# Latent attention in a two-layer trunk: two heads taken together, exponentials and values in fp32, the two heads' value matmuls on the two halves of the array's columns

## The chip, the cores and the metric

The kernel runs on one core of a Trainium2 chip. The metric is the time of the device for one launch, in microseconds (us), as the median of several runs of the same program. Engines are named as the profile names them: PE is TensorE (PEld its weight loads), DVE is VectorE, ACT is ScalarE, POOL is GpSimd, SP is SyncE, which here only issues transfers.

## The reference, cut to what matters

Two layers run for 1024 latent tokens and 128 context tokens. The first layer (windowed attention beside a state-space scan) is not touched. The second is multi-head latent attention with 16 heads: queries and keys have 64 plain and 32 rotated elements per head, values have 64.

```python
def dense_attention(q, k, v, scale, sink=None):          # one block of 128 queries after the other
    s = jnp.einsum("bqhgd,bkhd->bhgqk", qblk, k).astype(jnp.float32) * scale
    p = jax.nn.softmax(s, axis=-1)
    return jnp.einsum("bhgqk,bkhd->bqhgd", p.astype(v.dtype), v)

def mla_attend(q, k, v, g, w_out):
    out = dense_attention(q[:, :, :, None, :], k, v, MLA_SCALE)
    return (out.reshape(b, L, MLA_WIDTH) * jax.nn.silu(g)) @ w_out
```

Latent queries see 1024 latent and 128 cached context keys (nine tiles of 128 keys); the 128 context queries see 128 context keys of their own. All inputs and outputs are float32.

## The kernel before, in words

TensorE takes two formats here. A *float32r* operand is rounded to the precision of one pass through the array. Where more is needed the kernel keeps a value as two such parts, hi and lo, with hi + lo equal to the value, and adds two or three products (`mm3`, L256 to L258, is hi·hi + hi·lo + lo·hi). A plain *fp32* operand is split by the machine itself: each fp32 matmul of the program stands in the trace as two MATMUL records with two weight loads.

Latent attention works head by head. Four operand sets (`AK`, `BK`, `AQ`, `BQ`: hi and lo of keys and queries, elements by tokens) hold two pairs of heads. For a head, `head_max` (L1428) first makes the scores' row maxima from a one-pass product `pp`, 24 products of 128 queries by 384 keys and one of 128, each reduced by a DVE TENSOR_REDUCE (shown as L209, the line of a helper) in the step after; the negated maximum goes by DMA into row 96 of `AQ`, so that the score product subtracts it.

`head_main` then walks the queries in chunks of 512, 512 and 128, and in a chunk the tiles of 128 keys. One *step* is one tile of keys of one head: three score matmuls (L1449 to L1451) into a PSUM bank `sc` of the ring `pre` (two banks); on ACT two exponentials of that bank, one rounded to float32r (`ph`, L1458) and one in fp32 (`pf`, L1459); on DVE `pl = pf - ph` (L1473); on POOL the running sum of `pf` for the denominator (L1477). One step later come two value matmuls (L1467, L1468), `V·ph` and `V·pl`, into one bank `acco`. `V` holds 64 hi and 64 lo columns, so that the bank's upper 64 rows are the part that belongs to the lo columns. At the end of a chunk `gather` adds the two halves of the bank (ACT copy L1489, DVE add L1490), sums the denominator over the partitions with a product by ones (`den`, L1496, fp32, one weight column), inverts it by way of DRAM, and multiplies by the gate.

Beside the steps run pieces of work for the next pair of heads: `operands` (projections by `mm3` into the other two operand sets, `place`), `quad_weights`, `quad_rope`, `quad_values` every fourth head, and `head_max`. `spread` deals them out over the steps, at most three or four PSUM banks (`mm`, `tr`) a step, and `Steps` puts off what follows. While one head of a pair is worked on, the maxima of the following head are made.

The code's order is not the final order. The tile framework orders the instructions of each engine by its own simulation of the program (`schedule_with_timeline_sim=True` at the end of the file) within the dependencies. Only what goes through `pinned` stays behind the instructions given to its engine before. Each engine then works strictly in the order so found.

SBUF is four large tiles, R, S, G, F (`Memory`), from which named rings of buffers are cut.

Of the kernel before, what the change touches and what calls it, by code (L numbers as in the profile page):

```python
# [20 lines left out]
D = 1024  # L21
# [59 lines left out]
class Segment:  # L81
    """columns of one SBUF tile, handed out and taken back while the kernel is traced"""
# [27 lines left out]
class Memory:  # L110
    """four tiles of SBUF: R holds operands of float32r products, F everything else, S and G either by turns"""
# [26 lines left out]
class Space:  # L138
    """named rings of buffers in the memory"""
# [53 lines left out]
class Steps:  # L193
    """pieces of work put off by a number of steps of the stream that they go along with"""
# [26 lines left out]
def hybrid_trunk(ctx: ExitStack, tc: tile.TileContext, I, O, dbg=None, stage=99):  # L221
# [23 lines left out]
    def split(hi, lo, src, scale=None, lo_eng=None):  # L245
        """hi + lo == src * scale exactly; scale is None, a power of two or a [P, 1] operand."""
        lo_eng = lo_eng or dve
        if scale is None:
            act.copy(hi, src)  # L249
            lo_eng.tensor_tensor(lo, src, hi.bitcast(F32), ALU.subtract)  # L250
# [92 lines left out]
    def modulation(sp, l, j, parts):  # L343
        """columns 256 j .. 256 j + 255 of the map of layer l; whole weights, or split ones where TensorE has no time to spare"""
# [43 lines left out]
    def rstd_of(p, ssq, n, width):  # L388
        """ssq [128, width] -> (ssq / n + eps) ** -0.5"""
# [11 lines left out]
    def weave(main, n_main, aux, n_aux):  # L401
        """n_aux steps of aux spread evenly over n_main steps of main"""
# [300 lines left out]
    def fm_proj(w, b, hT, c):  # L703
        """128 columns of a slab for a chunk of tokens, columns by tokens"""
# [66 lines left out]
    def chunk_states(p, fb, xt, Bt):  # L771
        """states of two heads before every chunk, forward ones at rows 0..63, backward ones, counted from the last chunk, below"""
# [271 lines left out]
    def norm_T(p, l, cond, xh, tok):  # L1044
        """modulated transpose of a normalised token tile"""
# [10 lines left out]
    def residual(p, half, acc, x, gate, adder=pool):  # L1056
        """x[:, half] += gate * acc"""
# [212 lines left out]
    def pinned(f, *a):  # L1270
        """an instruction that stays behind those that its engine was given before"""
# [4 lines left out]
    def spare(name):  # L1276
        """a bank, to be read in the next step"""
# [6 lines left out]
    def until(n):  # L1284
        """waits for the n-th step from now"""
# [49 lines left out]
    def quad_rope(Q):  # L1335
        """the rotated parts of four heads' queries"""
        qh, ql = quads[Q][0]
        rh = p7.tile([128, T], F32R, tag="qrh", name="qrh", at="G")
        rl = p7.tile([128, T], F32R, tag="qrl", name="qrl", at="G")
# [47 lines left out]
    def operands(pair):  # L1387
        """fills the operand sets of a pair of heads"""
# [11 lines left out]
    def head_max(h):  # L1400
        """row of -max of the scores, a group of query tiles at a time"""
# [35 lines left out]
    def head_main(h, op, chunks=CHUNKS):  # L1437
        """a step per tile of keys: its scores and exponentials; the values of the tile before"""
        s, a = h % NSET, h % 2
        for q0, n, kts in chunks:  # L1440
            qs = slice(q0, q0 + n)
            acc = []
            last = chunks is not CHUNKS
            total = p7.tile([128, n if last else 512], F32, tag=f"pt{n if last else 512}", name="pt1", bufs=2)[:, 0:n]
            first = None
            for i, kt in enumerate(kts):
                sc = psum("pre", "sc")
                ks = slice(kt * 128, (kt + 1) * 128)
                pe.matmul(sc[:, 0:n], AK[s][0:96, ks], BQ[s][:, qs], start=True, stop=False)  # L1449
                pe.matmul(sc[:, 0:n], BK[s][:, ks], AQ[s][0:96, qs], start=False, stop=False)  # L1450
                pe.matmul(sc[:, 0:n], AK[s][:, ks], AQ[s][:, qs], start=False, stop=True)  # L1451
                if behind:
                    behind[0]()
                steps.tick()
                pf = p7.tile([128, 512], F32, tag="pf", name="pf", bufs=3)[:, 0:n]
                ph = p7.tile([128, 512], F32R, tag="ph", name="ph", bufs=3)[:, 0:n]
                pl = p7.tile([128, 512], F32R, tag="pl", name="pl", bufs=2)[:, 0:n]
                act.activation(ph, sc[:, 0:n], AF.Exp, scale=SCALE_M)  # L1458
                act.activation(pf, sc[:, 0:n], AF.Exp, scale=SCALE_M)  # L1459
                yield  # L1460
# [3 lines left out]
                def values(V=quads[h // 4][2][h // 2 % 2][:, kt, a], ph=ph, pl=pl, acc=acc, total=total, i=i, last=i == len(kts) - 1, q0=q0, n=n):  # L1464
                    if i == 0:
                        acc.append(psum("o", "acco")[:, 0:n])
                    pe.matmul(acc[0], V, ph, start=(i == 0), stop=False)  # L1467
                    pe.matmul(acc[0], V, pl, start=False, stop=last)  # L1468
                    if last:
                        after(1, gather, h, op, q0, n, acc[0], total)  # L1470

                def rest(pf=pf, ph=ph, pl=pl, total=total, i=i, alone=len(kts) == 1, first=first, values=values):
                    dve.tensor_tensor(pl, pf, ph.bitcast(F32), ALU.subtract)  # L1473
                    if alone:
                        pool.tensor_copy(total, pf)
                    elif i > 0:
                        pool.tensor_tensor(total, first if i == 1 else total, pf, ALU.add)  # L1477
                    behind[0] = values
                behind.append(rest)
                first = pf  # L1480
# [3 lines left out]
    def gather(h, op, q0, n, acc, total):  # L1484
        """adds the two parts of a head's outputs; divides a pair of heads by the denominators, gates"""
        a, j = h % 2, h // 2
        qs = slice(q0, q0 + n)
        low = p7.tile([64, 512], F32, tag="ol1", name="ol1")[:, 0:n]
# [211 lines left out]
```

## Time and profile before

| what | before |
|---|---|
| median of 3 runs | 1939.34 us (1937.37 to 1945.99) |
| profiled execution: span from first to last instruction (the page has no other time of it) | 1936.3 us |
| what lies between that span and the median | 3.0 us |
| PE busy, share of the span | 1770.5 us, 91% |
| DVE busy | 1338.3 us, 69% |
| ACT busy | 972.3 us, 50% |
| POOL busy | 849.1 us, 44% |
| the latent attention's steps: first score to last denominator | about 1140 to 1838 us, 698 us |
| in that stretch: PE, DVE, ACT, POOL busy | 625.61, 647.57, 444.40, 451.75 us |
| granted TensorE clock in that stretch | 0.95 |

In views of instructions a row gives the line, engine and operation, `out<-in`, shapes and the count, then busy time and mean ns of one. A matmul's duration holds its way through the array as well, so neighbours overlap: what one costs PE is the distance from its start to the next one's start, which the view in order of time gives. That view merges neighbours of one kind into a row with a count.

### The profile page before, as it was taken

Reading aid. Unit: us, or ns where it says so; the run is one execution under the profiler, and the core shown is the slowest. Engines: PE = TensorE matmul, PEld = TensorE weight load, DVE = VectorE, ACT = ScalarE, POOL = GpSimd, SP = SyncE. Lnnn points to the kernel's source line nnn. Section 1 sums busy time; section 2 is a strip of 40 time slices with the busy share of each in tenths; the row PEclk is TensorE's granted clock in tenths of the full one; section 3 lists DMA queues with packets and bytes.
Section 4 is the critical chain, followed back from the end, with each engine's and each line's share of the span. In section 5 each row is a group of like instructions: output and inputs, shape, how many; then the busy total and the mean of one; then the engine's idle time right before and its main releaser. Section 6 shows DMA issues by size and latency. Waiting matters only on the chain. (4 is left out here: it accounts for less than half of the span.)

```text
span 1936.3 us, 28171 instructions
## 1 busy us (share of the span) xinstructions
PE 1770.5 (91%) x9031; PEld 1405.9 (73%) x9031; DVE 1338.3 (69%) x2421; ACT 972.3 (50%) x2201; POOL 849.1 (44%) x781
## 2 busy tenths in 40 slices
PE   7899999999987898989999999998989899988898
PEld 3899999868766866767788986666666566654586
DVE  5666455654544577676654359999999899999833
ACT  5533224655654454444344236666567566765521
POOL 3410000233443346566340105866775586765632
PEclk9999999999988888989999989999989899998999
DMA  7333333343436786554535320211120121112352
GB/s 256 111 91 111 93 105 104 118 121 98 127 110 186 232 262 212 167 185 157 170 89 177 107 64 12 60 27 38 33 60 19 40 63 30 33 40 89 91 168 87
DMA packets 210664, 210.33 MB, mean 109 GB/s; under 512 B 36162, under 2 KB 175504, under 8 KB 210516
## 3 DMA queue, kind: packets, MB, share of 16 engines
q1 hardware_dynamic: 210372, 208.40, 35.7%
q8 instruction: 72, 1.18, 0.3%
q14 instruction: 76, 0.62, 0.1%
q0 software_dynamic: 144, 0.13, 0.0%
HBM read 151.94 MB, written 51.72 MB: 105 GB/s over the span
## 5 line engine op out<-in xcount | busy, mean ns | idle before, releaser
L1477 POOL TENSOR_TENSOR arenaF<-arenaF 128x512 f32<-128x512 f32 x256 | 390.9, 1528 | 171.4 <-PE den L1496 96.0
L256 PE MATMUL acc<-arenaR 128*128 128x384 f32 (+4 forms) x1152 | 390.6, 340 | 14.4 <-ACT arenaR L252 4.7
L257 PE MATMUL acc<-arenaR 128*128 128x384 f32 (+3 forms) x1080 | 362.7, 336 | 0.1
L258 PE MATMUL acc<-arenaR 128*128 128x384 f32 (+4 forms) x1056 | 352.1, 335 | 0.8 <-DVE arenaR L250 0.6
L256 PEld LDWEIGHTS acc<-arenaR 128*128 128x128 f32 x1152 | 224.3, 195 | 41.2 <-issue 7.0
L209 DVE TENSOR_REDUCE arenaF<-pp 128x1 f32<-128x384 f32 (+1 forms) x400 | 204.0, 534 | 21.6 <-PE pp L1428 18.9
L257 PEld LDWEIGHTS acc<-arenaR 128*128 128x128 f32 x1080 | 210.0, 194 | 10.7 <-issue 1.8
L258 PEld LDWEIGHTS acc<-arenaR 128*128 128x128 f32 x1056 | 206.0, 195 | 13.2 <-issue 3.0
L1473 DVE TENSOR_TENSOR arenaG<-arenaF,arenaS 128x512 fp32r<-128x512 f32 (+1 forms) x202 | 200.0, 996 | 3.9 <-PE acco L1468 2.7
L1459 ACT ACTIVATE arenaF<-sc 128x512 f32<-128x512 f32 (+1 forms) x304 | 174.3, 576 | 7.3 <-POOL arenaF L1477 6.7
L1468 PE MATMUL acco<-arenaG 128*128 128x512 f32 (+1 forms) x304 | 134.1, 444 | 42.9 <-DVE arenaG L1473 38.5
L1458 ACT ACTIVATE arenaS<-sc 128x512 fp32r<-128x512 f32 (+1 forms) x202 | 117.3, 582 | 91.0 <-PE sc L1451 46.1
L1005 ACT ACTIVATE arenaG<-arenaG,arenaF 128x128 f32<-128x128 f32 x288 | 88.4, 389 | 115.9 <-POOL arenaG L1003 115.4
L250 DVE TENSOR_TENSOR arenaR<-arenaF,arenaR 128x512 fp32r<-128x512 f32 (+2 forms) x135 | 115.3, 869 | 41.9 <-ACT arenaR L249 35.5
L249 ACT CAST arenaR<-arenaF 128x512 fp32r<-128x512 f32 (+3 forms) x151 | 91.6, 625 | 81.2 <-DMA arenaF<-in_ab_w_in_dram 19.1
L1468 PEld LDWEIGHTS acco<-arenaG 128*128 128x128 f32 x304 | 59.5, 196 | 98.7 <-DVE arenaG L1473 88.1
L258 PE MATMUL acc<-arenaR,arenaS 128*128 128x512 f32 (+1 forms) x336 | 128.9, 387 | 0.0
L749 POOL TENSOR_TENSOR arenaG<-arenaF,arenaG 128x512 fp32r<-128x512 f32 x28 | 48.6, 1734 | 151.4 <-PE acco L753 83.4
L1428 PE MATMUL pp<-arenaR 96*128 96x384 f32 x300 | 104.3, 385 | 8.4 <-DVE arenaF L209 4.2
L256 PE MATMUL acc<-arenaR,arenaS 128*128 128x512 f32 (+1 forms) x264 | 106.3, 403 | 1.0 <-ACT arenaS L249 0.7
L257 PE MATMUL acc<-arenaR,arenaS 128*128 128x512 f32 (+1 forms) x264 | 105.4, 399 | 0.0
L1449 PE MATMUL sc<-arenaR 96*128 96x512 f32 (+1 forms) x228 | 96.5, 423 | 7.1 <-ACT arenaF L1459 6.9
(339 smaller groups left out, 4052.9 us busy)
## 6 DMA issues: line engine op xcount, KB each, us to landing
arenaF<-in_ada_w_dram SPq DMA_DIRECT2D x96, 256.0 KB
arenaG<-cum_d SPq DMA_DIRECT2D x36, 512.0 KB
arenaF<-in_ab_w_in_dram SPq DMA_DIRECT2D x51, 256.0 KB
z_d<-arenaF SPq DMA_DIRECT2D x36, 128.0 KB
xs_d<-arenaF SPq DMA_DIRECT2D x8, 576.0 KB
arenaF<-xs_d SPq DMA_DIRECT2D x9, 512.0 KB
arenaF<-z_d SPq DMA_DIRECT2D x9, 512.0 KB
x_d<-arenaG SPq DMA_DIRECT2D x9, 512.0 KB
```

What stands on the lines that cost most here:

```text
L209: f()
L250: lo_eng.tensor_tensor(lo, src, hi.bitcast(F32), ALU.subtract)
L256: pe.matmul(out, ah, bh, start=first, stop=False)
L257: pe.matmul(out, ah, bl, start=False, stop=False)
L258: pe.matmul(out, al, bh, start=False, stop=last)
L1428: pe.matmul(pp[:, 0:w], AQ[s][0:96, t * 128:(t + 1) * 128], AK[s][0:96, k0:k0 + w], start=True, stop=True)
L1449: pe.matmul(sc[:, 0:n], AK[s][0:96, ks], BQ[s][:, qs], start=True, stop=False)
L1458: act.activation(ph, sc[:, 0:n], AF.Exp, scale=SCALE_M)
L1459: act.activation(pf, sc[:, 0:n], AF.Exp, scale=SCALE_M)
L1468: pe.matmul(acc[0], V, pl, start=False, stop=last)
L1473: dve.tensor_tensor(pl, pf, ph.bitcast(F32), ALU.subtract)
L1477: pool.tensor_tensor(total, first if i == 1 else total, pf, ALU.add)
```

## The change

- `head_main` becomes `pair_main`: a step is still one tile of keys of one head, but the two heads of a pair alternate, tile by tile.
- One exponential a step is left, in fp32 (L1455 of the changed file). The rounded one and the DVE subtraction are gone.
- `V` is kept in fp32: 64 columns a head. `quad_values` copies it out of PSUM with one ACT copy where it made a hi and a lo part.
- The value product is one fp32 matmul a step (L1465) in place of two float32r ones. The first head's goes to rows 0 to 63 of the bank `acco`, the second head's to rows 64 to 127: 64 columns of the array each. The code writes the two one behind the other, once per tile of keys of the pair.
- `gather` works once per pair and chunk: one ACT copy of the whole bank, no DVE add; the denominators of both heads go to rows 0 and 64 of one bank. The product of gate and reciprocal moves from POOL to DVE. For the short chunk POOL's copy is gone.
- The maxima of the next pair's two heads both come from the 12th step of a pair's 36 on, and those of the first pair's two heads both ahead of the first step (before: 19 of 50 products ahead).
- Buffers: `pf` six deep in G, which is set to fp32; `vv` half as wide, the rotated queries in F, and the residual stage's input ring in G.

The core of the diff:

```diff
         for pr in range(2):
-            tiles.append(p7.tile([128, NKT, 2, 128], F32R, tag="vv", name="vv", bufs=3, at="G"))
+            tiles.append(p7.tile([128, NKT, 2, 64], F32, tag="vv", name="vv", bufs=3, at="G"))
...
             for pr in range(2):
-                v = tiles[pr][:, kt]
-                after(1, split, v[:, :, 0:64], v[:, :, 64:128], acc[:, pr * 128:(pr + 1) * 128].rearrange("p (a d) -> p a d", a=2))
+                after(1, act.copy, tiles[pr][:, kt], acc[:, pr * 128:(pr + 1) * 128].rearrange("p (a d) -> p a d", a=2))
...
-                act.activation(ph, sc[:, 0:n], AF.Exp, scale=SCALE_M)
-                act.activation(pf, sc[:, 0:n], AF.Exp, scale=SCALE_M)
-                yield
+                for a in range(2):
+                    s = (2 * j + a) % NSET
+                    sc = psum("pre", "sc")
+                    pe.matmul(sc[:, 0:n], AK[s][0:96, ks], BQ[s][:, qs], start=True, stop=False)
+                    pe.matmul(sc[:, 0:n], BK[s][:, ks], AQ[s][0:96, qs], start=False, stop=False)
+                    pe.matmul(sc[:, 0:n], AK[s][:, ks], AQ[s][:, qs], start=False, stop=True)
+                    if a == 0 and behind:
+                        behind[0]()
+                    steps.tick()
+                    pf = p7.tile([128, 512], F32, tag="pf", name="pf", bufs=6, at="G")[:, 0:n]
+                    act.activation(pf, sc[:, 0:n], AF.Exp, scale=SCALE_M)
+                    pfs.append(pf)
+                    yield
...
-                    pe.matmul(acc[0], V, ph, start=(i == 0), stop=False)
-                    pe.matmul(acc[0], V, pl, start=False, stop=last)
+                    for a in range(2):
+                        pe.matmul(acc[0][a * 64:(a + 1) * 64], V[:, a], pfs[a], start=(i == 0), stop=last)
...
-                    dve.tensor_tensor(pl, pf, ph.bitcast(F32), ALU.subtract)
...
-        low = p7.tile([64, 512], F32, tag="ol1", name="ol1")[:, 0:n]
-        act.copy(low, acc[64:128])
-        dve.tensor_tensor(op[a * 64:(a + 1) * 64, qs], acc[0:64], low, ALU.add)
+        act.copy(op[:, qs], acc)
...
-                pe.matmul(den[0:1, 0:n], ones, total, start=True, stop=True)
+            for a in range(2):
+                pe.matmul(den[a * 64:a * 64 + 1, 0:n], ones, totals[a], start=True, stop=True)
...
-            after(2, pinned, pool.tensor_tensor, gt, gt, rb, ALU.mult)
+            after(2, pinned, dve.tensor_tensor, gt, gt, rb, ALU.mult)
...
+            aux = [(chain(*make), n_make, 0), (chain(head_max(2 * pair + 2), head_max(2 * pair + 3)), 2 * NMAX, 11)]
```

How the framework's order moves on PE. First, the middle of a pair, before. `sc` are score banks, `acco` the value bank, `pp` the products for the maxima; the sizes are output partitions by columns:

```order
L1428 MATMUL pp<-arenaR 128x384
L1449 MATMUL sc<-arenaR 128x512
L1450 MATMUL sc<-arenaR 128x512
L1451 MATMUL sc<-arenaR 128x512
L1468 MATMUL acco<-arenaG 128x512
L1467 MATMUL acco<-arenaS,arenaG 128x512
L1468 MATMUL acco<-arenaG 128x512
L1467 MATMUL acco<-arenaR,arenaG 128x512
```

The same place in the changed kernel, here with the buffers' numbers, so that both value matmuls are seen to write the one accumulator 10507:

```order
L1448 MATMUL sc_10578<-arenaR_63 128x512
L1449 MATMUL sc_10578<-arenaR_63 128x512
L1450 MATMUL sc_10578<-arenaR_63 128x512
L1465 MATMUL acco_10507<-arenaG_10198 64x512
L1427 MATMUL pp_10604<-arenaR_63 128x384
L1427 MATMUL pp_10621<-arenaR_63 128x384
L1448 MATMUL sc_10592<-arenaR_63 128x512
L1449 MATMUL sc_10592<-arenaR_63 128x512
L1450 MATMUL sc_10592<-arenaR_63 128x512
L1465 MATMUL acco_10507<-arenaG_10198 64x512
```

The value matmuls of the two heads, neighbours in the code, come apart: each stands alone between score products of the full width. Over the whole program 304 such matmuls are left where 608 stood, and only three of them, in one place near the end, stand side by side.

Second, PE just ahead of the steps, where the first pair's maxima are made. Before:

```order
L1428 MATMUL pp<-arenaR 128x384
L1467 MATMUL acco<-arenaR,arenaG 128x512
L1428 MATMUL pp<-arenaR 128x128
L1449 MATMUL sc<-arenaR 128x512
L1450 MATMUL sc<-arenaR 128x512
L1451 MATMUL sc<-arenaR 128x512
L1428 MATMUL pp<-arenaR 128x384
L1449 MATMUL sc<-arenaR 128x512
L1450 MATMUL sc<-arenaR 128x512
L1451 MATMUL sc<-arenaR 128x512
L1468 MATMUL acco<-arenaG 128x512
```

And in the changed kernel:

```order
L1465 MATMUL acco<-arenaG 64x512
L1427 MATMUL pp<-arenaR 128x384
L1412 MATMUL pt<-ident,arenaF 1x128
L1427 MATMUL pp<-arenaR 128x384 x2
L1448 MATMUL sc<-arenaR 128x512
L1449 MATMUL sc<-arenaR 128x512
L1427 MATMUL pp<-arenaR 128x384 x11
L1412 MATMUL pt<-ident,arenaF 4x128
L1427 MATMUL pp<-arenaR 128x384 x8
```

Ahead of the second value matmul stand 26 products `pp` before, and all 50 of the first pair in the changed kernel.

More of the change, by code (lines that the diff above doesn't have):

```diff
@@ L1435, in hybrid_trunk, with pair_main @@
     behind = []
-    def head_main(h, op, chunks=CHUNKS):
-        s, a = h % NSET, h % 2
+    def pair_main(j, op, chunks=CHUNKS):
+        tails = chunks is not CHUNKS
         for q0, n, kts in chunks:
             qs = slice(q0, q0 + n)
[L1442 to L1445, printed above, removed]
+            acc, totals, first = [], [None, None], [None, None]
@@ L1469, in values @@
                     if last:
[L1470 to L1477, printed above, removed]
+                        after(1, gather, j, op, q0, n, acc[0], totals)
@@ new lines, in rest @@
+                def rest(pfs=pfs, totals=totals, i=i, alone=len(kts) == 1, first=first, values=values, n=n):
+                    for a in range(2):
+                        if alone:
+                            totals[a] = pfs[a]
+                        elif i == 0:
+                            first[a] = pfs[a]
+                        else:
+                            if i == 1:
+                                totals[a] = p7.tile([128, 512], F32, tag="pt", name="pt1", bufs=4, at="G")[:, 0:n]
+                            pool.tensor_tensor(totals[a], first[a] if i == 1 else totals[a], pfs[a], ALU.add)
@@ L1478, in rest, with gather @@
                     behind[0] = values
                 behind.append(rest)
-                first = pf
     ending = []
-    def gather(h, op, q0, n, acc, total):
-        a, j = h % 2, h // 2
+    def gather(j, op, q0, n, acc, totals):
         qs = slice(q0, q0 + n)
-        low = p7.tile([64, 512], F32, tag="ol1", name="ol1")[:, 0:n]
-        act.copy(low, acc[64:128])
-        dve.tensor_tensor(op[a * 64:(a + 1) * 64, qs], acc[0:64], low, ALU.add)
-        dn = p7.tile([64, 8], F32, tag="dn1", name="dn1", bufs=3)[:, 0:n // 64]
-        flat = rd1_d[h, qs].rearrange("(p c) -> p c", p=64)
+        act.copy(op[:, qs], acc)
+        dn = p7.tile([128, 8], F32, tag="dn1", name="dn1", bufs=3)[:, 0:n // 64]
+        flat = [rd1_d[2 * j + a, qs].rearrange("(p c) -> p c", p=64) for a in range(2)]
@@ L1494, in sums @@
         def sums():
             den = spare("den")
-            pe.matmul(den[0:1, 0:n], ones, total, start=True, stop=True)
+            for a in range(2):
+                pe.matmul(den[a * 64:a * 64 + 1, 0:n], ones, totals[a], start=True, stop=True)
             after(1, store, den)
         def store(den):
-            row = p7.tile([1, 512], F32, tag="dr1", name="dr1", bufs=2)[:, 0:n]
-            act.copy(row, den[0:1, 0:n])
-            dma.dma_start(rd1_d[h:h + 1, qs], row)
-            after(2, pinned, dma.dma_start, dn, flat)
+            row = p7.tile([65, 512], F32, tag="dr1", name="dr1", bufs=2)[:, 0:n]
@@ L1504, in store @@
+            for a in range(2):
+                act.copy(row[a * 64:a * 64 + 1], den[a * 64:a * 64 + 1, 0:n])
+                dma.dma_start(rd1_d[2 * j + a:2 * j + a + 1, qs], row[a * 64:a * 64 + 1])
+            for a in range(2):
+                after(2, pinned, dma.dma_start, dn[a * 64:(a + 1) * 64], flat[a])
             after(4, invert)
@@ L1507, in invert @@
             pinned(dve.reciprocal, dn, dn)
-            dma.dma_start(flat, dn)
-            if a == 1:
-                after(2, fetch)
+            for a in range(2):
+                dma.dma_start(flat[a], dn[a * 64:(a + 1) * 64])
+            after(2, fetch)
         def fetch():
@@ L1543, in final_vectors @@
         dma.dma_start(fw, bcast_rows(I["final_norm_w"], 128))
[L1544 removed]
+        gates[0:] = [fw, load_gate(p8, 1, 0)]
     gates = []
@@ L1551, in spread @@
         for i in range(n_main):
-            for k, (g, n) in enumerate(aux):
-                while done[k] * n_main < n * (i + 1) and taken.count(steps.now) < 3 and next(g, None) != "wait":
+            for k, (g, n, i0) in enumerate(aux):
+                while i >= i0 and done[k] * (n_main - i0) < n * (i + 1 - i0) and taken.count(steps.now) < 3 and next(g, None) != "wait":
                     done[k] += 1
             yield
-        for g, _ in aux:
+        for g, _, _ in aux:
             for _ in g:
@@ L1579, in hybrid_trunk @@
     wp.close()
+    mem.set("G", F32)
     while len(AK) < NSET:
         operand_set()
-    rows0 = head_max(0)
-    for stream in (first, quad_values(0), islice(rows0, 19)):
+    rows1 = head_max(1)
+    for stream in (first, quad_values(0), head_max(0), rows1):
         for _ in stream:
```

68 lines of the change are left out of this document (23 added, 45 removed).

## The prediction

> **What bounds the kernel now.** I read first the stretch of the latent attention in the view of windows, since nothing else in the program changes, then the costliest groups and the waits inside it, and then PE in order of time, to learn what one matmul costs PE.
>
> ```profile
> core 0: us, PE busy (x) PEld busy (x) DVE busy (x) ACT busy (x) POOL busy (x), PEclk, DMA share, GB/s
> 1140.00:1838.00 698.00, 625.61 (x2510) 431.96 (x2510) 647.57 (x1138) 444.40 (x954) 451.75 (x315) 0.95 0.17 45
> 1140.00:1160.00 20.00, 17.25 (x60) 12.12 (x60) 16.33 (x43) 6.53 (x22) 1.16 (x1) 0.71 0.16 41
> ```
>
> DVE is busy 93% of 698 us, PE 90%. But a PE row's busy time holds a matmul's way through the array, so PE may be far from full. The groups and the waits of this stretch:
>
> ```profile
> L209 DVE TENSOR_REDUCE arenaF<-pp 128x1 f32<-128x384 f32 x384 | 200.2, 545 | 21.6 <-PE pp L1428 18.9
> L1473 DVE TENSOR_TENSOR arenaG<-arenaF,arenaS 128x512 fp32r<-128x512 f32 x192 | 197.1, 1032 | 3.9 <-PE acco L1468 2.7 <-ACT arenaF L1459 1.1
> L1473 DVE TENSOR_TENSOR arenaG<-arenaF,arenaR 128x512 fp32r<-128x512 f32 x96 | 98.4, 1025 | 1.8 <-PE acco L1468 1.4 <-ACT arenaF L1459 0.2
> L1490 DVE TENSOR_TENSOR arenaF<-acco,arenaF 64x512 f32<-64x512 f32 x32 | 21.7, 679 | 1.5 <-ACT arenaF L1489 1.1
> L250 DVE TENSOR_TENSOR arenaG<-acc,arenaG 128x128 fp32r<-128x128 f32 x76 | 20.4, 278 | 1.7 <-ACT arenaG L249 1.2
> L1458 ACT ACTIVATE arenaS<-sc 128x512 fp32r<-128x512 f32 x192 | 114.5, 598 | 88.1 <-PE sc L1451 44.7 <-DVE arenaG L1473 29.9 <-PE acco L1467 4.1
> L1458 ACT ACTIVATE arenaR<-sc 128x512 fp32r<-128x512 f32 x96 | 57.4, 598 | 42.5 <-PE sc L1451 21.1 <-DVE arenaG L1473 13.4 <-DVE arenaF L209 2.7
> ...
> PE acco L1468 <- DVE arenaG L1473: 38.5, 65, 1.9
> PE sc L1449 <- ACT arenaF L1459: 7.6, 15, 1.2
> PE pp L1428 <- DVE arenaF L209: 6.3, 16, 1.1
> PE pt L1413 <- DVE arenaF L1408: 3.3, 5, 2.5
> PE pp L1428 <- DVE arenaS L250: 2.5, 2, 1.2
> ```
>
> The subtraction L1473 is 295.5 us of DVE and the wait that PE, its weight loads and ACT meet most. So today DVE paces the steps.
>
> **PE's price list**, from PE in order of time. Float32r products of 512, 384 and 256 columns:
>
> ```profile
> 403.55 0.40 PE L753 MATMUL acco<-arenaG 128*65 128x512 f32 x1
> 403.78 0.40 PE L751 MATMUL acco<-arenaG 128*65 128x512 f32 x1
> 404.02 0.40 PE L752 MATMUL acco<-arenaG 128*64 128x512 f32 x1
> 404.25 0.33 PE L258 MATMUL acc<-arenaR 128*128 128x384 f32 x1
> ...
> 402.22 0.34 PE L256 MATMUL acc<-arenaR 128*128 128x384 f32 x1
> 402.40 0.33 PE L257 MATMUL acc<-arenaR 128*128 128x384 f32 x1
> ...
> 1140.06 0.28 PE L258 MATMUL acc<-arenaR 128*128 128x256 f32 x1
> 1140.18 0.28 PE L256 MATMUL acc<-arenaR 128*128 128x256 f32 x1
> ```
>
> Start to start that is 0.233 us (0.70 over three), 0.175 and 0.12. Using 64 of the array's columns changes nothing: 404.02 to 404.25.
>
> Now fp32. A lone fp32 matmul with one weight column (`den`), one with 128 (`off`, 64 rows), and four with the 64 columns that the change uses, but only 128 moving columns (`st`; an x4 row is two matmuls):
>
> ```profile
> 1313.16 0.40 PE L1467 MATMUL acco<-arenaS,arenaG 128*128 128x512 f32 x1
> 1313.49 1.02 PE L1496 MATMUL den<-arenaF 128*1 128x512 f32 x2
> 1314.44 0.50 PE L1449 MATMUL sc<-arenaS,arenaR 96*128 96x512 f32 x1
> 1314.77 0.39 PE L1450 MATMUL sc<-arenaS,arenaR 96*128 96x512 f32 x1
> ...
> 703.07 1.12 PE L992 MATMUL off<-arenaG,arenaF 64*128 64x512 f32 x2
> 704.12 0.32 PE L1011 MATMUL yacc<-arenaF,arenaG 128*128 128x64 f32 x1
> ...
> 391.50 0.34 PE L258 MATMUL acc<-arenaR 128*128 128x384 f32 x1
> 391.77 0.65 PE L808 MATMUL st<-arenaF 128*64 128x128 f32 x4
> 392.26 0.60 PE L808 MATMUL st<-arenaS,arenaF 128*64 128x128 f32 x4
> 392.79 0.45 PE L753 MATMUL acco<-arenaG 128*65 128x512 f32 x1
> 393.07 0.40 PE L751 MATMUL acco<-arenaG 128*65 128x512 f32 x1
> ```
>
> The fp32 matmul itself takes 0.95 us with 1 column, 1.05 with 128. Its neighbours pay too: the float32r product ahead of it needs 0.33 instead of 0.23 (1313.16 to 1313.49; 391.50 to 391.77 is 0.27 instead of 0.175), and so does the one behind it (1314.44 to 1314.77). So an *island* of one fp32 matmul among float32r costs 0.95 or 1.05, plus 0.10 and 0.10: 1.15 to 1.25. For 64 columns I take the middle, 1.20, because its rows show both gaps and a first weight load between the two.
>
> **PE's floor today.** The counts: 288 long steps (L1473's 192 + 96), 384 `pp` (L209), and for the projections three times
>
> ```profile
> L256 PE MATMUL acc<-arenaR 128*128 128x384 f32 x78 | 27.0, 346 | 1.8 <-DVE arenaF L209 1.5 <-DVE arenaF L1272 0.4
> L256 PE MATMUL acc<-arenaR 128*128 128x256 f32 x45 | 14.1, 312 | 0.1
> L256 PE MATMUL acc<-arenaR 128*128 128x512 f32 x26 | 12.0, 460 | 0.1
> ```
>
> 864 score and 576 value products at 0.233: 201 and 134. 384 `pp` at 0.175: 67. Projections, 234 at 0.175, 135 at 0.12, 78 at 0.233: 75. 32 `den` (16 heads, two long chunks) at 1.15: 37. The short chunk's and the transposes, by the same spacing: 12. Together 526 us. So in 698 us PE loses 172 us to waits and to half clock (mean 0.95).
>
> **The change, part by part.**
>
> *DVE* loses L1473 (295.5 us, with the short ones some 300), L1490 (some 25), the lo part of V (20), and gains the gate products, 24 at most at about 1 us or less: 648 falls to some 320. *ACT* loses L1458 (176): 444 falls to about 260. *POOL* keeps its 256 sums. All three end far below PE, so I cost these removals at nothing beyond the waits they end.
>
> *PE*: 576 float32r value products (134) become 288 fp32 matmuls. The changed order shows each alone between scores and `pp`, so each is an island: 288 x 1.20 = 346. The 16 short ones cost about 0.5 each against two of 0.07: +6. Scores, `pp`, projections and denominators are as many as before, but the two heads' denominators are now issued together, long and short: 24 islands fewer, 0.2 each, -5. Floor: 526 - 134 + 346 + 6 - 5 = 739 us. That alone is above today's 698. The gap to be filled by PE's own work is larger than what the end of all waits could return.
>
> The Trainium skill, "FP8 and Floating Point Precision", section TensorE Precision Notes, says that true FP32 makes 4 passes through the array. By four passes of 0.233 alone an fp32 matmul is estimated at 0.93, and the floor at 526 - 134 + 268 + 6 - 5 = 661; the rows of `den` and `off` show the passes and the gaps around them, so I go by the rows.
>
> *Ahead of the steps*: in 1140 to 1160 PE is full for about 10 of 20 us, DVE, with the reductions, for 16.33. Now 50 `pp` stand ahead of the second value matmul instead of 26. 24 more reductions at 0.545 are 13 us of DVE, with 6 us of PE's work beside them. PE's idle time there: 10 + 7 = 17.
>
> *Waits left in the steps*: the four waits above that do not name L1473 sum to 20 us; I keep 20. Bounds: 5, if faster DVE and ACT end them; 57, if PE also runs at clock 0.95 as now (5% of 739 is 37 more). Queue positions: the value matmul waits on an exponential made a step earlier (0.6 us of ACT against about 2.2 of PE); the score bank is free once that exponential is done; what waits behind it on PE are the scores of the other head.
>
> Sum: 739 + 17 + 20 = 776 us in place of 698, +78. The profiled span 1936.3 becomes 2014; the median of the runs shown, 1939.34, is 3.0 above it: **2017**. The model's weak term is the island: 0.10 off it is 29 us.
>
> **Rivals.**
>
> *The halves overlap.* The change's own idea. Two fp32 products on different *rows* of the array do overlap when they are neighbours:
>
> ```profile
> 687.17 0.33 PE L258 MATMUL acc<-arenaR 128*128 128x384 f32 x1
> 687.43 1.13 PE L992 MATMUL off<-arenaG,arenaF 64*128 64x512 f32 x4
> ```
>
> Two matmuls here take 1.13, where at 703.07 one took 1.12. If the column halves did so, a pair would cost 1.05 + 0.20 = 1.25: 144 x 1.25 = 180, floor 526 - 134 + 180 + 3 - 5 = 570, and with 37 of idle 607: 91 below 698, 1848 in all. Against it: in the order three score products stand between the halves, and only one place has neighbours. Decides if PE starts the second half ahead of the scores before it: 4%.
>
> The Trainium skill, "TensorEngine Tiling (Array Packing)", Key Properties, says that different tiles can execute weight loads and matmuls in parallel; the `off` rows agree for rows, no run here shows it for columns. The same skill, "TensorE: Matmul & The Clock Gate", Part 3, The mechanism, has matmuls in strict order: by that, halves apart cannot meet, and the sum stays.
>
> *The gaps vanish.* If the moving data of the scores could follow the half-width matmul closely, an island would be four passes, 4 x 0.233 = 0.93: floor 526 - 134 + 268 + 6 - 5 = 661, with 37 of idle 698: 1939, no change. For it: the 64-column float32r product has no gap. Against it: the 64-column `st` rows have both. 6%, of which 2 count as faster (fewer waits than 20) and 4 as the same.
>
> *PE keeps losing what it loses now.* If 172 us of waits and slow clock stay, because the framework's order was made for other prices (DVE's reductions now come two a step, from the 12th step on), the stretch is 739 + 172 = 911: 2152. Against it: DVE is at 320 of 739. 8%.
>
> **How the numbers follow.** Forecast 82%: own range 1973 to 2068. Its lower end is an island of 1.10 (-29) and waits of 5 (-15); its upper end waits of 57 (+37) and an island of 1.25 (+14). Rivals 4, 6 and 8%. Ends that need two misses at once leave little of it outside, so the range given, 1973 to 2068, leaves out the rivals and no more: about 2 in 10. A change of about 0.5% is what a measurement can tell from none: slower 0.90 (forecast and last rival), same 0.04, faster 0.06 (first rival, and a part of the second).
>
> **What would show it.** Right: value rows L1465 with 1.0 us to the next start, and 0.33 for the scores before and behind; DVE about 320 of some 780 us and PE's waits on DVE almost gone; clock near 1.0 in the stretch; L1448 and `pp` paced by PE. Wrong: two L1465 rows starting within 0.01 us of each other anywhere but at the end; a stretch below 739; a wait of PE on POOL or on `pf` buffers, which I hold for hidden (six buffers, POOL's sums 1.5 us for a step of 2.2).

## The result and the profile after

| | before | changed |
|---|---|---|
| median of 4 runs | 1938.36 us (1936.47 to 1945.99) | 1993.24 us (1992.55 to 1999.76) |
| ratio to before, 95% interval | | 1.0282 [1.0258, 1.0306] |
| span of the profiled execution | 1936.3 us | 1991.1 us |
| first score to last denominator | 698.4 us | 747.6 us |
| from the last denominator to the end | 100.1 us | 105.8 us |

The change makes the kernel 2.8% slower. The forecast was 2017 us, with 1973 to 2068 as its range.

The head of the changed kernel's page, busy time and share of the span for each engine, and its chain of waits by engine:

```profile
span 1991.1 us, 27076 instructions
...
PE 1887.9 (95%) x9031; PEld 1322.5 (66%) x9031; DVE 1028.8 (52%) x1989; ACT 823.7 (41%) x1873; POOL 738.6 (37%) x741
...
PE 76%; DMA 7%; DVE 5%; POOL 4%; issue 2%; ACT 1%; SPq 1%; POOLq 0%; DVEq 0%; ACTq 0%
```

PE is busy 117 us longer than before, DVE 310 us less. The stretch of the steps, in the view of windows (start and end, length, then busy time and count of PE, weight loads, DVE, ACT and POOL, the granted clock, DMA share, GB/s), the costliest groups in it, and the waits of PE:

```profile
1137.80:1885.40 747.60, 739.42 (x2482) 346.97 (x2480) 332.79 (x707) 294.90 (x627) 347.84 (x275) 0.99 0.15 41
```

```profile
L1478 POOL TENSOR_TENSOR arenaG<-arenaG 128x512 f32<-128x512 f32 x256 | 329.3, 1288 | 388.9 <-ACT arenaG L1455 317.0 <-ACT arenaF L1500 52.7 <-issue 18.3
L1465 PE MATMUL acco<-arenaG 128*64 128x512 f32 x576 | 309.3, 621 | 1.2 <-ACT arenaG L1455 1.2
L209 DVE TENSOR_REDUCE arenaF<-pp 128x1 f32<-128x384 f32 x384 | 198.3, 552 | 237.9 <-PE pp L1427 237.7
L1455 ACT ACTIVATE arenaG<-sc 128x512 f32<-128x512 f32 x288 | 171.5, 597 | 308.6 <-PE sc L1450 268.2 <-POOL arenaG L1478 39.8
```

```profile
PE pp L1427 <- DVE arenaF L209: 2.8, 8, 0.5
PE acco L1465 <- ACT arenaG L1455: 1.2, 3, 0.4
PE sc L1450 <- DMA arenaR<-arenaF: 1.0, 2, 0.6
PE sc L1448 <- ACT arenaG L1455: 0.7, 1, 0.7
```

Before, DVE was busy 93% of the stretch; now it is at 333 of 748 us and waits for PE, as ACT does, and POOL waits for ACT. PE waits for next to nobody: with two smaller rows its waits sum to 6.8 us. And it is PE in which the value matmuls became dearer. An x576 group for 288 matmuls says that an fp32 matmul is two records. In order of time:

```profile
1418.62 0.44 PE L1448 MATMUL sc<-arenaR 96*128 96x512 f32 x1
1418.90 0.40 PE L1449 MATMUL sc<-arenaR 96*128 96x512 f32 x1
1419.13 0.40 PE L1450 MATMUL sc<-arenaR 97*128 97x512 f32 x1
1419.46 1.07 PE L1465 MATMUL acco<-arenaG 128*64 128x512 f32 x2
1420.46 0.51 PE L1448 MATMUL sc<-arenaR 96*128 96x512 f32 x1
1420.81 0.40 PE L1449 MATMUL sc<-arenaR 96*128 96x512 f32 x1
```

The score ahead of the value matmul takes 0.33 us to the next start where its like takes 0.23, the value matmul 1.00, the score behind it 0.35 instead of 0.23. An island costs 1.00 + 0.10 + 0.12 in these rows, against 2 x 0.233 before. Over the 285 long value matmuls that stand alone the medians are 0.10 (what the product ahead takes beyond its like), 0.48 and 0.52 (the two records) and 0.11 (the product behind), 1.21 us in all. The expectations below were written with 1.195, and I go on counting with that. 288 times the difference is 210 us.

At the one place near the end where value matmuls are neighbours stands something else:

```profile
1880.25 1.93 PE L1465 MATMUL acco<-arenaG 128*64 128x512 f32 x6
1882.11 1.02 PE L1494 MATMUL den<-arenaG,arenaF 128*1 128x512 f32 x2
```

Six records, three matmuls, in 1.86 us, where apart they would take 3 us: two of them overlap. So the halves of the columns can work together, and the changed kernel's order keeps them from it.

### The profile page after: what moved, and what is told of

It is laid out like the page before. It is cut to its first block, busy times and chain, and to the rows that moved or that the text cites. A ratio compares the mean times of both kernels' runs of the same rounds, so it can differ in the third digit from the quotient of the medians.

```text
span 1991.1 us, 27076 instructions
## 1 busy us (share of the span) xinstructions
PE 1887.9 (95%) x9031; PEld 1322.5 (66%) x9031; DVE 1028.8 (52%) x1989; ACT 823.7 (41%) x1873; POOL 738.6 (37%) x741
## 4 chain that ended last, share of the span: by engine, by line
PE 76%; DMA 7%; DVE 5%; POOL 4%; issue 2%; ACT 1%; SPq 1%; POOLq 0%; DVEq 0%; ACTq 0%
PE acco L1465 15%; PE acc L256 12%; PE acc L258 11%; PE acc L257 11%; PE pp L1427 5%; PE sc L1448 4%; PE sc L1450 4%; PE sc L1449 3%; DMA arenaG<-rd_d 2%; DMA arenaG<-cum_d 2%; DVE arenaR L250 1%; PE st L808 1%; POOL arenaG L1003 1%; PE den L1494 1%; PE yacc L1011 1%
## 5 line engine op out<-in xcount | busy, mean ns | idle before, releaser
L1478 POOL TENSOR_TENSOR arenaG<-arenaG 128x512 f32<-128x512 f32 x256 | 329.3, 1288 | 388.9 <-ACT arenaG L1455 317.0
L256 PE MATMUL acc<-arenaR 128*128 128x384 f32 (+4 forms) x1248 | 430.1, 345 | 15.2 <-ACT arenaR L252 5.4
L258 PE MATMUL acc<-arenaR 128*128 128x384 f32 (+4 forms) x1152 | 388.0, 338 | 0.2
L1465 PE MATMUL acco<-arenaG 128*64 128x512 f32 (+1 forms) x608 | 316.2, 604 | 1.2 <-ACT arenaG L1455 1.2
L1455 ACT ACTIVATE arenaG<-sc 128x512 f32<-128x512 f32 (+1 forms) x304 | 175.9, 580 | 324.7 <-PE sc L1450 284.3
L1465 PEld LDWEIGHTS acco<-arenaG 128*64 128x64 f32 x608 | 58.1, 135 | 107.4 <-issue 100.9
L1427 PE MATMUL pp<-arenaR 96*128 96x384 f32 (+1 forms) x300 | 102.8, 406 | 3.1 <-DVE arenaF L209 2.8
L1448 PE MATMUL sc<-arenaR 96*128 96x512 f32 (+1 forms) x228 | 94.9, 416 | 0.7 <-ACT arenaG L1455 0.7
L1450 PE MATMUL sc<-arenaR 97*128 97x512 f32 (+1 forms) x228 | 90.1, 396 | 1.0 <-DMA arenaR<-arenaF 1.0
L258 PE MATMUL acc<-arenaR,arenaS 128*128 128x512 f32 (+1 forms) x240 | 90.2, 381 | 0.0
L1449 PE MATMUL sc<-arenaR 96*128 96x512 f32 (+1 forms) x228 | 88.8, 389 | 0.0
L1003 POOL TENSOR_SCALAR_AFFINE_SELECT arenaG<-arenaG 128x512 f32<-128x512 f32 x72 | 59.6, 851 | 66.2 <-DMA arenaG<-cum_d 57.2
```

Source lines behind the costliest of these rows:

```text
L256: pe.matmul(out, ah, bh, start=first, stop=False)
L258: pe.matmul(out, al, bh, start=False, stop=last)
L1427: pe.matmul(pp[:, 0:w], AQ[s][0:96, t * 128:(t + 1) * 128], AK[s][0:96, k0:k0 + w], start=True, stop=True)
L1465: pe.matmul(acc[0][a * 64:(a + 1) * 64], V[:, a], pfs[a], start=(i == 0), stop=last)
L1478: pool.tensor_tensor(totals[a], first[a] if i == 1 else totals[a], pfs[a], ALU.add)
```

## The experiments

My theory: PE is the bound; the value matmuls cost 1.2 us apiece because each stands alone; as neighbours, the two halves would overlap. Each part of it has a rival. Each run is compared with runs of the kernel before on the same chip; times are medians.

**What the subtraction had cost.** The kernel before, without L1473. It leaves out the low part of the exponentials (the rounded part enters the values twice), and is here for its time alone:

```diff
-                    pe.matmul(acc[0], V, pl, start=False, stop=last)
+                    pe.matmul(acc[0], V, ph, start=False, stop=last)
...
-                    dve.tensor_tensor(pl, pf, ph.bitcast(F32), ALU.subtract)
```

> The kernel before, without the subtraction L1473: the second value matmul of a step takes the rounded exponentials again, so the low part of the exponentials is left out of the values (they count twice). PE's work is unchanged, DVE has 300 us less. Theory A (of the 172 us that PE lost in the stretch before, most came from DVE's pace; the changed kernel got nearly all of it back and paid 213 us for it in fp32 islands): the stretch falls from 698 to 526 + 7 (waits as in the changed kernel) to + 40, 535 to 570, the time to 1775 to 1815 us. Theory B (those 172 us came from the framework's order, the clock or PSUM hand-offs, and the changed kernel lost them for the mere reason that its PE is full): the stretch stays above 650, the time above 1890 us.

Measured: 1825.13 us, ratio 0.9415 [0.9381, 0.9448]. The stretch by windows:

```profile
1137.80:1721.20 583.40, 560.80 (x2519) 430.17 (x2518) 392.55 (x835) 436.58 (x953) 377.70 (x316) 0.98 0.21 55
```

583 us in place of 698: the subtraction's pace held back 115 us, two thirds of what PE lost. Theory A's mechanism, though the stretch is 13 us and the time 10 us above its upper ends: PE still loses 57 us over its counted 526 (22 in waits, some 12 to a granted clock of 0.98; the rest is not settled). The changed kernel freed DVE as well and stands at 747.6, 164 us above this run. By the count its work is 200 us more (210 for the long value matmuls, 6 for the short ones, 16 less for the denominators, see below); over its count it loses 22 us, 35 less than this run.

**Neighbours.** The changed kernel; the first head's matmul is held until it follows the second head's at once:

```diff
-                    for a in range(2):
-                        pe.matmul(acc[0][a * 64:(a + 1) * 64], V[:, a], pfs[a], start=(i == 0), stop=last)
+                    pe.matmul(acc[0][64:128], V[:, 1], pfs[1], start=(i == 0), stop=last)
+                    tc.keep_in_program_order(pe.matmul(acc[0][0:64], V[:, 0], pfs[0], start=(i == 0), stop=last))
```

> The changed kernel, with the two value matmuls of a pair of steps kept as neighbours in PE's order: the first head's is held until it can follow the second head's at once. Everything is computed as before. Theory A (the column halves overlap, but only for neighbours, as the two denominators and three rows near the end of the changed kernel's trace show them, 7 ns apart): 288 islands of 1.195 us become 144 pairs of about 1.05 + 0.20 = 1.25 us, 344 - 180 = 164 us less work on PE. The stretch of the steps falls from 746 to about 580 to 620 us (DVE at 331 and POOL at 348 are still below that), the time to 1830 to 1870 us. Theory B (the column halves do not overlap for 64-column values, the 7 ns were the small case): a pair costs 0.48 + 0.52 twice plus one pair of gaps, 2.2 us; only 144 x 0.20 = 29 us go, the time is about 1965 us. What tells them apart: L1465 rows 7 ns apart against 1.0 us apart.

Measured: 1852.13 us, ratio 0.9547 [0.9521, 0.9573]: 141 us below the changed kernel and 4.5% below the kernel before. PE in order of time, and the stretch:

```profile
1406.07 0.39 PE L1450 MATMUL sc<-arenaS,arenaR 97*128 97x512 f32 x1
1406.39 0.64 PE L1464 MATMUL acco<-arenaG 128*64 128x512 f32 x1
1406.40 0.64 PE L1465 MATMUL acco<-arenaG 128*64 128x512 f32 x1
1406.87 0.59 PE L1464 MATMUL acco<-arenaG 128*64 128x512 f32 x1
1406.88 0.59 PE L1465 MATMUL acco<-arenaG 128*64 128x512 f32 x1
1407.40 0.50 PE L1448 MATMUL sc<-arenaR 96*128 96x512 f32 x1
1407.74 0.39 PE L1449 MATMUL sc<-arenaR 96*128 96x512 f32 x1
```

```profile
1137.80:1747.40 609.60, 586.29 (x2519) 340.50 (x2518) 352.73 (x710) 291.48 (x629) 350.28 (x276) 0.96 0.19 53
```

The rows of L1464 and L1465 start 0.01 us apart, record by record. Two value matmuls take 1.01 us (1406.39 to 1407.40), and with the gaps 1.21, which is what one took before. Counted: 144 x (2 x 1.195 - 1.21) = 170 us less on PE. The stretch fell by 138. PE's waits rose from 7 to some 23 us, and the granted clock fell from 0.99 to 0.96, 3% of 610 or 18 us; that is the rest.

**Columns or neighbours?** The same, with both heads on columns 0 to 63, into two banks:

```diff
-                        acc.append(psum("o", "acco")[:, 0:n])
+                        acc.extend(psum("o", "acco")[:, 0:n] for _ in range(2))
...
+                    pe.matmul(acc[1][0:64], V[:, 1], pfs[1], start=(i == 0), stop=last)
+                    tc.keep_in_program_order(pe.matmul(acc[0][0:64], V[:, 0], pfs[0], start=(i == 0), stop=last))
...
-        act.copy(op[:, qs], acc)
+        for a in range(2):
+            act.copy(op[a * 64:(a + 1) * 64, qs], acc[a][0:64])
```

> As the kernel with neighbours, but both heads' values go through the same 64 columns of the array, into two banks in place of two halves of one (both banks of that ring, so a chunk's accumulators are not double buffered any more; one ACT copy more for each pair and chunk). All is computed. Theory A (the overlap comes from the two halves of the columns): no overlap here, a pair costs 2 x 1.0 + 0.20 = 2.2 us, the time is 1955 to 1980 us. Theory B (neighbouring fp32 matmuls overlap wherever they lie in the array, or the 7 ns have another reason): the time equals that of the kernel with neighbours on two halves.

Measured: 1959.46 us, ratio 1.009 [1.0057, 1.0124]. PE in order of time:

```profile
1404.29 1.07 PE L1464 MATMUL acco<-arenaG 128*64 128x512 f32 x2
1405.20 1.02 PE L1465 MATMUL acco<-arenaG 128*64 128x512 f32 x2
1406.15 0.44 PE L256 MATMUL acc<-arenaR 128*128 128x384 f32 x1
```

One behind the other, 1.86 us for the two. But this run also has other banks than the run before it, so one more differs from it by the columns alone:

```diff
-                    pe.matmul(acc[1][0:64], V[:, 1], pfs[1], start=(i == 0), stop=last)
+                    pe.matmul(acc[1][64:128], V[:, 1], pfs[1], start=(i == 0), stop=last)
```

(and the copy takes rows 64 to 127 of that bank).

> As the run with both heads on columns 0 to 63, with the same two banks and the same extra copy, but the second head's values on columns 64 to 127. Everything is computed. It differs from that run by the columns alone and from the run with neighbouring halves by the banks alone. Theory A (the overlap belongs to the halves of the columns): the rows come in pairs 7 ns apart, and the time is that of the neighbouring halves, 1852 us, plus what the two banks cost (one ACT copy more for a pair and chunk, no second accumulator): 1855 to 1885 us. Theory B (it needs both halves to write one bank, and that is why the run on columns 0 to 63 was slow): records about 0.43 to 0.52 us apart, 1950 to 1965 us as there.

Measured: 1854.06 us, ratio 0.9544 [0.9519, 0.9569], as fast as the halves in one bank, with the rows in pairs again:

```profile
1401.64 0.64 PE L1464 MATMUL acco<-arenaG 128*64 128x512 f32 x1
1401.65 0.64 PE L1465 MATMUL acco<-arenaG 128*64 128x512 f32 x1
```

So it is the halves of the columns, and the missing second accumulator costs nothing that shows in the time. The Trainium skill, "TensorE: Matmul & The Clock Gate", section Why this matters for your kernels, says that small products whose outputs lie in distinct column groups run concurrently; with neighbours the rows agree, at 0.01 us between starts.

**The denominators.** The changed kernel makes the two heads' one-column products side by side, at columns 0 and 64. Here both go to column 0, of two banks:

```diff
-            den = spare("den")
+            den = [spare("den") for _ in range(2)]
             for a in range(2):
-                pe.matmul(den[a * 64:a * 64 + 1, 0:n], ones, totals[a], start=True, stop=True)
+                pe.matmul(den[a][0:1, 0:n], ones, totals[a], start=True, stop=True)
...
```

> The changed kernel, with the two heads' denominators in two banks, both at row and column 0 of the array, in place of rows 0 and 64 of one bank. All is computed. Theory A (the two one-column denominators overlap since they lie in different halves of the columns, and this saved about 15 us): their rows stand some 0.95 us apart in place of 7 ns, 16 long ones add 16 x 0.95 = 15 us, the time is about 2008 us. Theory B (they overlap as neighbours of one column whatever the columns, or the saving is elsewhere): no change from 1993 us.

Measured: 2002.36 us, ratio 1.0318 [1.0287, 1.0348], 9 us above the changed kernel (7 by the two ratios). The two intervals overlap, so the rows decide. The changed kernel, and then this run, at the same place of the program:

```profile
1271.65 1.03 PE L1494 MATMUL den<-arenaG,arenaF 128*1 128x512 f32 x4
1272.61 0.50 PE L256 MATMUL acc<-arenaR 128*128 128x512 f32 x1
```

```profile
1271.61 1.88 PE L1494 MATMUL den<-arenaG,arenaF 128*1 128x512 f32 x4
1273.41 0.50 PE L256 MATMUL acc<-arenaR 128*128 128x512 f32 x1
```

0.96 us for both denominators against 1.80. Summed from start to start over the stretch, the long denominators take 18.5 us in the one and 29.6 in the other: their overlap saves 11 us, not the 15 expected.

**What makes an island dear?** In the run on columns 0 to 63 neighbours took 0.93 us each, and still the gaps stood around them. Are the gaps the passage between fp32 and float32r, or between the full width of the array and half of it? The two-bank kernel, each matmul at full width, with the value columns of both heads:

```diff
-                    pe.matmul(acc[1][64:128], V[:, 1], pfs[1], start=(i == 0), stop=last)
+                    pe.matmul(acc[1], V.rearrange("p a d -> p (a d)"), pfs[1], start=(i == 0), stop=last)
```

(the other head likewise)

> As the run with two banks and neighbours, but each head's value matmul takes the value columns of both heads, 128 of the array's columns, with that head's exponentials; half of what it makes is not read. All results are computed. So every matmul of the step is fp32 or float32r at full width, and no product uses a half of the array. Theory A (the 0.10 us that the float32r products ahead of and behind a value matmul lose come from the passage between fp32 and float32r): the gaps stand as in the run on columns 0 to 63, 0.33 ahead, 0.33 behind, some 1.9 us between, and the time is that run's, 1945 to 1970 us. Theory B (the gaps come from the change between the full width and half of it): no gaps here, the pair is 4 x 0.43 = 1.72 us, 144 x 0.35 = 50 us are gone, the time is 1900 to 1920 us.

Measured: 1925.88 us, ratio 0.9927 [0.9902, 0.9953], 34 us below the run on columns 0 to 63: theory B, with two thirds of its 50 us, so that the time lies 6 us above its range; PE waits 9 us more than in that run (22 against 13). PE in order of time:

```profile
1405.01 0.40 PE L1450 MATMUL sc<-arenaR 97*128 97x512 f32 x1
1405.24 1.02 PE L1464 MATMUL acco<-arenaG 128*128 128x512 f32 x2
1406.11 1.02 PE L1465 MATMUL acco<-arenaG 128*128 128x512 f32 x2
```

The score ahead takes 0.23 us where it took 0.33, and the first value matmul 0.87. Then the same width with the changed kernel's own order, the heads apart (two banks and their copies as above):

```diff
-                        pe.matmul(acc[0][a * 64:(a + 1) * 64], V[:, a], pfs[a], start=(i == 0), stop=last)
+                        pe.matmul(acc[a], V.rearrange("p a d -> p (a d)"), pfs[a], start=(i == 0), stop=last)
```

> The changed kernel, its value matmuls apart in PE's order as they are there, but each over 128 columns of the array (the value columns of both heads, of whose products half is not read), into two banks. All results are computed. Theory A (what an island pays beyond four times 0.215 us is the change between full and half width, so a full-width fp32 matmul costs 0.86 us among float32r products, wherever it stands): 288 x (1.195 - 0.86) = 96 us less on PE than in the changed kernel, 1895 to 1925 us, below the kernel before and near the run with full-width neighbours. Theory B (full width helped only because the two were neighbours, and apart each still pays its gaps): 288 x 0.2 of gaps stay, 1980 to 2000 us. The rows tell them apart: 0.23 or 0.33 from the score product ahead to the value matmul, 0.86 or 1.0 for that one.

Measured: 1926.77 us, ratio 0.9898 [0.986, 0.9936]. PE in order of time, and the stretch:

```profile
1404.56 0.40 PE L1450 MATMUL sc<-arenaR 97*128 97x512 f32 x1
1404.80 1.02 PE L1465 MATMUL acco<-arenaG 128*128 128x512 f32 x2
1405.26 0.74 PE L1427 MATMUL pp<-arenaR,arenaS 96*128 96x384 f32 x1
1405.84 0.39 PE L1448 MATMUL sc<-arenaR 96*128 96x512 f32 x1
```

```profile
1137.80:1828.40 690.60, 671.48 (x2567) 442.51 (x2566) 345.03 (x714) 303.78 (x655) 351.82 (x276) 0.97 0.17 47
```

The score ahead takes 0.24 us: no gap. The `pp` behind is put down as starting early and lasting long; by the next start, 1404.80 to 1405.84, the value matmul and one `pp` of 0.175 take 1.04 us, so the value matmul takes 0.865 and the `pp` pays nothing. What differs from 1.195 is the width, and the two banks, which cost nothing above. A matmul of twice the width, half of it wasted, costs PE 0.33 us less. The same kernel gets 66 us faster, is 1% faster than the kernel before, and takes as long as the run at full width with neighbours (1925.88): without the change of width it does not matter where the value matmuls stand.

The Trainium skill, "TensorEngine Tiling (Array Packing)", Key Properties, says that a change of the tiling mode drains TensorE. These rows agree, and put the price of a change there and back at 0.33 us. The float32r products with 64 columns (L752, in the prediction) show no such gap.

The weight loads show where the time goes. The first one of a value matmul, in the changed kernel (its matmul starts at 1419.46) and in this run (at 1404.80):

```profile
1419.46 0.19 PEld L1465 LDWEIGHTS acco<-arenaG 128*64 128x64 f32 x2 [0.37 <-issue]
```

```profile
1404.57 0.42 PEld L1465 LDWEIGHTS acco<-arenaG 128*128 128x128 f32 x2
```

At full width the weights load 0.23 us ahead, beside the score product that still runs; at half width the load and its matmul start together. So it is in the changed kernel at each change of width, there or back: at all 561 changes between a value matmul and a score, `pp` or projection product behind the lead-in, the load stands 1 or 2 ns ahead of its matmul. The second load of a half-width matmul, where the width does not change, stands 0.43 us ahead (median). How much of the 0.33 us is the load itself and how much the end of the product ahead is not separated.

The counted 96 us became 66. In the profiled executions it is 57 in the stretch, and 63 for the same work, since this run does ahead of the last denominator 6 us of projection products that the changed kernel does behind it. Of the 33 that are missing, 14 are the granted clock, 0.97 against 0.99 of 691 us, and 11 are waits of PE, 18 us against 7; 8 stay open. The time lies 2 us outside the expected range.

**Larger groups.** If the change of width is paid once for each group, then four value matmuls together (two heads, two tiles of keys) should save more:

```diff
...
+                    held.append((V, pfs))
+                    if i % 2 or last:
+                        for k, (V, pfs) in enumerate(reversed(held)):
+                            for a in (1, 0):
+                                m = pe.matmul(acc[0][a * 64:(a + 1) * 64], V[:, a], pfs[a], start=(i < 2 and k == 0), stop=last and k == len(held) - 1)
+                                if a == 0 or k:
+                                    tc.keep_in_program_order(m)
+                        del held[:]
```

> The kernel with neighbouring halves, with the values of two tiles of keys held until all four matmuls (two heads, two tiles) can stand side by side: per long chunk five groups in place of nine pairs. Everything is computed. Six buffers of exponentials as before, four of them now held by a group. Theory A (the 0.20 us around an fp32 matmul are paid once for each entry into fp32 and back, not for each matmul): 16 long chunks x 4 entries fewer x 0.20 = 13 us less than with pairs, 1839 us, if the six buffers still let the exponentials run ahead. Theory B (the gap belongs to each matmul): no change from 1852 us. Theory C (the buffers bind: the exponentials of the next tile must wait for the group): ACT waits on PE's value matmuls, PE waits on exponentials, the time is 1870 us or more.

> The same groups of four, with eight buffers of exponentials in place of six (one input ring of the residual stage moves to another part of SBUF to make room). Everything is computed. Theory A: 1839 us, with PE's waits on exponentials as in the kernel with pairs (about 1 us in all). If six buffers bind, this run is faster than the run with six by what PE waits there; if they do not, the two are the same within 0.3%.

Measured: six buffers 1861.88 us, ratio 0.9606 [0.9578, 0.9633]; eight buffers 1846.08 us, ratio 0.9526 [0.9497, 0.9554]. With eight:

```profile
1401.82 0.40 PE L1450 MATMUL sc<-arenaS,arenaR 97*128 97x512 f32 x1
1402.15 1.94 PE L1468 MATMUL acco<-arenaG 128*64 128x512 f32 x8
1404.01 0.62 PE L1427 MATMUL pp<-arenaR 96*128 96x384 f32 x2
```

A group of four takes 1.86 us, and 2.06 with its gaps, where two pairs took 2.42: 64 groups save 23 us of PE. Yet the time is 6 us less than with pairs, within both intervals, so no gain is shown. The two strongest waits of PE in the stretch, with six buffers and then with eight:

```profile
PE pp L1427 <- DVE arenaF L209: 17.6, 13, 3.0
PE sc L1448 <- ACT arenaG L1455: 10.3, 11, 5.8
```

```profile
PE pp L1427 <- DVE arenaF L209: 12.3, 12, 2.8
PE sc L1448 <- ACT arenaG L1455: 6.8, 12, 1.4
```

With pairs these were 8.8 and 2.3 us. Six buffers cost 16 us against eight, so they bind, as theory C has it, though not with its 1870. Of its mechanism the trace shows PE's longer waits on exponentials (10.3 us against 6.8), but no wait of ACT on a value matmul. With eight, PE's waits of all kinds sum to 31 us against 23 with pairs, which takes 8 of the 23 us, and the granted clock is 0.95 against 0.96, some 6 us; where the rest went is not settled.

## Why the prediction was right, and where it was off

**The bound.** Right. PE's waits on DVE's subtraction vanished, PE became the bound, and the steps run at PE's own pace. (That ACT met the subtraction most was misread: in the two rows of L1458 its waits on PE's scores, 65.8 us, come ahead of those on the subtraction, 43.3. The sum does not use it.) Of the 172 us that I said PE lost, the run without the subtraction gives back 115.

**The island, 1.20 us.** Right in size, 1.195, and with it the direction. But I put its gaps down to fp32 among float32r, and that is wrong: at full width an fp32 matmul among float32r costs 0.865 and has no gap. All three kinds of row from which I took the price (`den` with 1 column, `off` with 64 rows, `st` with 64 columns) are fp32 *and* use a part of the array; I could not tell the two apart and did not say so. The price would have been wrong for a change to full-width fp32. My rival in which the gaps vanish gave 661 us of work and 1939. It did not come true at half width; the full-width run has the islands without gaps that it assumed, at 0.865 in place of 0.93, and takes 1926.77.

**The halves apart.** Right: in the steps they do not meet, as the order showed. The rival's own sum, an overlapping pair at 1.25 and 1848 us, is what the run with neighbours gives: 1.21 and 1852.13. The 4% stood on the order, rightly.

**The denominators, -5.** Too small by 11 us. I counted the shared gaps of the two heads' products that now stand together, and not that at columns 0 and 64 they are the very case of the rival: neighbours on two halves. The rows of the run with both at column 0 show it.

**Waits left, 20.** Measured 7: 13 us off. The four waits that I carried over all but end with faster DVE and ACT, as the lower bound of 5 had it. The upper bound added the clock of before, 0.95, as a price of its own; the clock rose to 0.99 as the waits went.

**The lead-in, 17 idle.** In 1137.8 to 1172.4 us PE made 48 `pp` in 23.2 us from start to start, 14.8 more than 48 x 0.175. About right, though not all of it is idle: the granted clock was 0.75 there.

**Engines.** DVE 320 forecast, 333 measured; ACT 260 against 295, 35 too low, of no consequence. POOL's sums, held at 1.5 us, took 1.29. That the `pf` buffers stay hidden was right: ACT waited 39.8 us for POOL's sums, which read them (the row of L1455), but PE waited on those exponentials for 1.9 us in all.

**The sum.** Island 288 x 0.005 = 1 less, denominators 11 less, waits 13 less: 776 becomes 751. Measured 747.6, and the last denominator now stands ahead of some 25 projection products (0.227 each, 6 us) that had been done by then before, so that the tail is 5.7 us longer. That move is missing in the prediction, but changes only where the time is counted. +78 forecast, +54.8 measured in the span: the difference is the denominators' overlap and the waits.

## What to carry to other kernels

Two fp32 products on different halves of the array's columns overlapped here only as neighbours in PE's final order: look at that order, and if a scheduler separates them, hold the earlier one back until the later is ready; here this turned +2.8% into -4.5%. An fp32 product that uses half of the columns, alone among full-width ones, pays for the change of width there and back; if it can have no partner, full width with wasted columns may be cheaper. When you take a price from a row, list every way in which that row differs from its neighbours before you name the cause.

## What I had not expected

- **The change of width costs 0.33 us there and back, and the change between fp32 and float32r nothing that shows**: 1.195 us for an fp32 value matmul on 64 columns, 0.865 on 128.
- **Even one-column products overlap** as neighbours, if they lie in different halves of the columns: 0.96 us for two denominators against 1.80.
- **POOL's sum got faster without being touched.** The groups before, and in the run without the subtraction:

```profile
L1477 POOL TENSOR_TENSOR arenaF<-arenaF 128x512 f32<-128x512 f32 x256 | 390.9, 1528 | 171.4 <-PE den L1496 96.0 <-ACT arenaF L1459 57.7 <-ACT arenaS L1458 2.6
```

```profile
L1476 POOL TENSOR_TENSOR arenaF<-arenaF 128x512 f32<-128x512 f32 x256 | 331.5, 1295 | 148.8 <-ACT arenaF L1459 103.1 <-PE den L1495 24.4 <-ACT arenaF L1500 6.4
```

  The same 256 sums take 1528 ns beside DVE's subtractions and 1295 without them (1288 in the changed kernel). DVE's two-operand work slows POOL's; through what is not shown.
- **The granted clock went with PE's waits.** Over the stretch it was 0.95 before, 0.99 in the changed kernel, 0.98 without the subtraction, 0.96 with neighbours, 0.97 at full width. Each hundredth is some 6 us, so that the two faster arrangements of the changed kernel lost 14 to 18 us of their gain to it. In the trace these are falls to 0.50 for 3.4 us or a multiple of it. Behind the lead-in, from 1176 us to the last denominator, PE sat idle for 68 us before, and the clock fell 13 times; for 20 us and 4 times with neighbours; for 16 us and 4 times with the heads apart at full width; for 4 us and not once in the changed kernel. In the 8 us ahead of each of these falls PE had been idle for 1.2 us or more. So a wait of PE is paid twice, once as idle time and once as clock, as far as the order of events tells; no run changed the idle time alone.
